# LayerNorm row sums out of the last PSUM addition, squares on ScalarE, and a new planned order, in a two-layer decoder trunk

## The chip, the cores and the metric

The kernel runs on one core of one Trainium2 chip. The metric is the device time of one launch in microseconds (us); a smaller one is better. The engines are TensorE (PE in the profile, its weight loads PEld), VectorE (DVE), ScalarE (ACT), GpSimd (POOL) and SyncE (SP, which issues nearly all transfers). "Span" is the time from the first to the last event of one profiled execution; that execution's own time is slightly longer.

## The reference, cut to what matters

512 tokens of width 1024 go through two layers. Layer 0 is a block-sparse attention with eight heads, layer 1 a gated DeltaNet with eight heads. Each layer modulates its input, projects it, mixes tokens, projects back, and ends in a LayerNorm over the residual:

```python
for i in range(2):
    mod = silu(c) @ ada_w[i] + ada_b[i]
    shift, scale, gate = split(mod, 3)
    h = x * (1 + scale) + shift
    y = moba_branch(h, ...) if i == 0 else gdn_branch(h, ...)
    x = layer_norm(4 ** 0.25 * x + gate * y, ln_g[i], ln_b[i])

def layer_norm(x, g, b):
    mu = mean(x); var = mean((x - mu) ** 2)
    return (x - mu) * rsqrt(var + 1e-5) * g + b
```

Everything is float32. The change is to how `mu` and `var` are computed, in both layer norms.

## The kernel before

**Tiling.** The residual `xn` stays in SBUF as four slices of 128 tokens (`st` = 0 to 3), each 128 partitions by 1024 numbers. A matmul in full precision is made of three passes with operands cut into a high and a low part (`wh`, `wl` of the weights, `hH`, `hL` of the activations). Projections land in PSUM banks of 128 x 512. `g2` is the half of the 1024 columns.

**The planner.** Every piece of work is a Python generator that yields the engine it wants, an estimated cost and the time at which its input is there. The class `Weave` picks the piece that can start first, and among equal ones that with the lowest rank. The table `PLACE` gives a rank to each piece by name; `RANK` holds ranks of groups, and six numbers `pool_...` by which work that may run on DVE or POOL is kept away from POOL: one twentieth of the number is added, in us, to POOL's end. `InOrder` fixes the order that results, so each engine runs a list that was decided ahead of the launch, and an instruction that waits holds all that stand behind it on its engine. The planner's estimates decide only the order; the chip decides the times.

**End of layer 0 and the norm between the layers.** `out0` (line 966) runs the output projection; slices 0 and 1 are made of two parts (`ya` for heads 0 to 5, `yb` for heads 6 and 7), slices 2 and 3 of one (`ya`). For each PSUM bank `evac` (line 884) multiplies by the gate row and adds to `xn`, both on DVE. `norm0` (line 922) then normalises a slice: `norm_stats` (line 905) runs `bn_stats` on each half of 512 columns on DVE, joins the two with `bn_aggr`, adds epsilon on DVE; `root` raises to the power of -0.5 on POOL; then two DVE operations, one for each half, subtract the mean and scale. `mod_t` transposes two normalised slices on PE (`h_ps`), applies layer 1's modulation (`ht`, on DVE and ACT) and cuts the result into `hH` (ACT) and `hL`. Its first half (`hf` = 0) is slices 0 and 1. `residual` afterwards scales and shifts `xn` for the residual of layer 1.

**Layer 1.** `proj1` takes the weights in the order of `order1`: z0 in two halves, q0, k0, v0, q1, v1 and so on, then the output projection in four parts (o0 to o3), each for two heads. `conv` runs a convolution over four taps and a SiLU on each projection (tiles `qc`, `kc`, `vc`), mostly on DVE. `decays` computes the decay factors, with a round trip through memory. `inverse(p)` starts from transposes of `kc` (`kt_ps`) and the decays and computes a triangular inverse for a pair of heads. `evac` adds each part of the output projection to `xn`: names `y0` to `y3`.

**The final norm.** `finish` (line 1776) handles a slice once all its parts are added. For slices 0 and 1 (`ACT_STATS = 2`) the sum is taken on ACT with a Copy that also writes out its row sum, and the squares with a Square pass on ACT; both dump their result in the slice's output buffer `f`. Slices 2 and 3 use `norm_stats` with `bn_stats` on DVE. Slices 0 to 2 are then normalised on ACT in halves and multiplied by g and shifted by b on DVE (or POOL); slice 3 takes two three-operand DVE operations for each half. `store` writes each half out.

Of the kernel before, what the change touches and what calls it, by code (L numbers as in the profile page):

```python
# [30 lines left out]
def flat(ap, dims, offset=0):  # L31
# [4 lines left out]
RANK = dict(pool_cut=42.445, pool_gate=32.272, pool_w=67.056, pool_mod=23.224, pool_res=0.0, pool_fin=0.0, fetch=22, kv0=50, qk0=45, kv00=40, cols2=20, mods=50, loads=25, evac0=96, conv0=17, decays=11, evac1=60, zs=49, conv=45, prep=8, resid=0, decay_f=67, inverse=4, inner=0, queries=40, values=94, recur=96, gated=7, keep0=43, norm0=37, mod_t=58, cut0=75, cut1=78)  # L36

PLACE = {
# [27 lines left out]
    "mod_t_1_2": -117.243, "mod_t_1_3": -977.754, "prep": 142.937, "residual": 134.202, "decays": -63.77,  # L66
# [30 lines left out]
}  # L97


def name_of(piece):  # L100

    code, given = piece.gi_code, piece.gi_frame.f_locals
    words = [code.co_name]
    for v in code.co_varnames[:code.co_argcount] + tuple(v for v in code.co_freevars if v == "st"):
        x = given.get(v)
        if isinstance(x, range):
            words.append(str(x[0]))
# [146 lines left out]
def act(n, ptr=0, acc=0):  # L254
    return 0.1 + 0.00083 * n + 0.09 * ptr + 0.1 * acc
# [12 lines left out]
def trunk(ctx: ExitStack, tc: tile.TileContext, x, c, ada_w, ada_b, ln_g, ln_b, moba_w_in, moba_w_out,  # L268
# [611 lines left out]
    pl.add(RANK["loads"], mod_loads())  # L880
    pl.add(100, proj0())


    def evac(o, st, g2, name, first_, e):
        gs = slice(g2 * 512, g2 * 512 + 512)
        if first_ is False:
# [982 lines left out]
```

## Time and profile before

| | us |
|---|---|
| median of three timed runs | 647.38 (646.84 to 647.98) |
| the profiled execution | 646.1 |
| its span | 644.4 |
| PE busy in the span | 614.2 |
| DVE busy | 484.1 |
| ACT busy | 346.2 |
| POOL busy | 46.7 |

All sums below are made against the profiled execution. Busy times of PE are modelled at the ends of matmuls. A duration printed for an operation is a little longer than the step by which its engine's queue advances, since the next one starts before the last one's end. Nearly all instructions carry one line number, that of the helper that records them, so the tiles' names tell them apart: `lnst`, `lnmv`, `lnve` are the statistics, `lnsq` the sums on ACT, `nb` the product of mean and reciprocal deviation, `fin` the buffer `f`.

### The profile page before, as it was taken

What the parts mean: (1) busy time and instruction counts of PE and PEld (TensorE: products, weight loads), DVE (VectorE), ACT (ScalarE), POOL (GpSimd) and SP (SyncE); (2) the same over time, 40 slices, a digit from 0 to 9 for tenths busy, and PEclk for the clock granted to TensorE, in tenths of its full rate; (3) what the DMA queues carried; (4) which work ended last, traced back from release to release, by engine and by line L of the source; (5) the groups of instructions that cost most, each with busy time, mean ns of one, the idle gap of its engine ahead of it and who ended that gap; (6) DMA issues with size and microseconds to landing.
All of it is one profiled execution on the core that took longest, in us unless ns stands there. A gap on an engine that the chain in (4) does not pass through costs nothing.

```text
span 644.4 us, 11258 instructions
## 1 busy us (share of the span) xinstructions
PE 614.2 (95%) x4214; PEld 519.0 (81%) x4214; DVE 484.1 (75%) x1099; ACT 346.2 (54%) x873; POOL 46.7 (7%) x65
## 2 busy tenths in 40 slices
PE   7999999999999999999889998899999999999992
PEld 6888788988888898888888886688878878887781
DVE  4796786775766468688889768857865986898877
ACT  1345764453544157204345595597589579745571
POOL 0000000000000000010300030010020021002011
PEclk8999999999999999999999998999999999999997
DMA  9995645455554335422313625344222423511203
GB/s 254 303 307 167 219 158 164 131 164 167 164 177 147 131 131 183 144 74 66 99 46 89 144 56 145 89 99 109 65 70 80 124 67 99 140 34 68 97 1 131
DMA packets 80969, 82.20 MB, mean 128 GB/s; under 512 B 8761, under 2 KB 67346, under 8 KB 80402
## 3 DMA queue, kind: packets, MB, share of 16 engines
q1 hardware_dynamic: 80834, 81.45, 43.3%
q8 instruction: 33, 0.54, 0.3%
q14 instruction: 22, 0.18, 0.1%
q10 hardware_dynamic: 80, 0.03, 0.0%
HBM read 78.82 MB, written 2.65 MB: 126 GB/s over the span
## 4 chain that ended last, share of the span: by engine, by line
PE 76%; DVE 9%; ACT 6%; DMA 4%; issue 2%; SPq 1%; DVEq 0%; ACTq 0%
PE z_ps L244 12%; PE y_ps L244 11%; PE gq_ps L244 7%; PE gk_ps L244 6%; PE v_ps L244 5%; PE k_ps L244 5%; PE q_ps L244 5%; PE gz_ps L244 4%; PE gv_ps L244 4%; PE s_ps L244 3%; PE o_ps L244 3%; DMA aw<-in_ada_w_dram 2%; PE os_ps L244 2%; PE kq_ps L244 2%; DVE xn L244 2%
## 5 line engine op out<-in xcount | busy, mean ns | idle before, releaser
L244 DVE SCALAR_TENSOR_TENSOR acc<-ga,cs,acc 128x512 f32<-128x512 f32 x56 | 40.3, 745 | 14.1 <-DMA ga<-in_ada_w_dram 14.1
L244 ACT ACTIVATE pr<-s_ps,nm 128x256 f32<-128x256 f32 (+1 forms) x48 | 20.6, 436 | 30.3 <-DVE nm L244 30.2
L244 DVE TENSOR_REDUCE nm<-s_ps 128x1 f32<-128x256 f32 (+1 forms) x64 | 22.0, 382 | 17.9 <-PE s_ps L244 17.9
L244 PE MATMUL gq_ps<-hH,wh_1q 128*128 128x512 f32 (+1 forms) x80 | 29.3, 366 | 0.0
L244 PE MATMUL gk_ps<-hH,wh_1k 128*128 128x512 f32 x64 | 26.8, 419 | 1.9 <-ACT wh_1k L244 1.3
L244 PE MATMUL v_ps<-wh_0v,hH 128*128 128x256 f32 x96 | 28.3, 295 | 0.0
L244 PE MATMUL gq_ps<-hL,wh_1q 128*128 128x512 f32 (+1 forms) x80 | 27.9, 348 | 0.0
L244 PE MATMUL gq_ps<-hH,wl_1q 128*128 128x512 f32 (+1 forms) x80 | 27.8, 348 | 0.0
L244 PE MATMUL z_ps<-hH,wh_0z 128*128 128x512 f32 x64 | 27.1, 424 | 0.7 <-ACT qT L244 0.7
L244 PE MATMUL y_ps<-wh_1o,ogh 128*128 128x512 f32 x64 | 27.1, 424 | 0.0
L244 PE MATMUL v_ps<-wh_0v,hL 128*128 128x256 f32 x96 | 27.1, 282 | 0.0
L244 PE MATMUL v_ps<-wl_0v,hH 128*128 128x256 f32 x96 | 27.1, 282 | 0.0
L244 PE MATMUL gk_ps<-hH,wl_1k 128*128 128x512 f32 x64 | 25.9, 404 | 1.3 <-DVE wl_1k L244 1.3
L244 DVE TENSOR_SCALAR nm<-nm 128x1 f32<-128x1 f32 x128 | 23.8, 189 | 4.1 <-ACT pr L244 1.1
L244 PE MATMUL gv_ps<-hH,wh_1v 128*128 128x512 f32 x64 | 26.6, 416 | 0.0
L244 DVE TENSOR_TENSOR xn<-xn,y_ps 128x512 f32<-128x512 f32 x34 | 23.2, 682 | 4.5 <-PE y_ps L244 4.2
L244 PE MATMUL gk_ps<-hL,wh_1k 128*128 128x512 f32 x64 | 25.5, 399 | 0.0
L244 PE MATMUL y_ps<-wh_0o,oH 128*128 128x512 f32 x64 | 25.5, 398 | 0.0
L244 PE MATMUL y_ps<-wl_1o,ogh 128*128 128x512 f32 x64 | 25.3, 395 | 0.0
L244 PE MATMUL y_ps<-wh_1o,ogl 128*128 128x512 f32 x64 | 25.2, 394 | 0.0
L244 PE MATMUL z_ps<-hL,wh_0z 128*128 128x512 f32 x64 | 25.2, 394 | 0.0
L244 PE MATMUL gv_ps<-hL,wh_1v 128*128 128x512 f32 x64 | 25.1, 392 | 0.0
(331 smaller groups left out, 1987.8 us busy)
## 6 DMA issues: line engine op xcount, KB each, us to landing
ga<-in_ada_w_dram SPq DMA_DIRECT2D x64, 256.0 KB
aw<-in_ada_w_dram SPq DMA_DIRECT2D x14, 512.0 KB
raw_0z<-in_moba_w_in_dram SPq DMA_DIRECT2D x8, 512.0 KB
raw_0o<-in_moba_w_out_dram SPq DMA_DIRECT2D x8, 512.0 KB
raw_1z<-in_gdn_w_in_dram SPq DMA_DIRECT2D x8, 512.0 KB
raw_1q<-in_gdn_w_in_dram SPq DMA_DIRECT2D x8, 512.0 KB
raw_1k<-in_gdn_w_in_dram SPq DMA_DIRECT2D x8, 512.0 KB
raw_1v<-in_gdn_w_in_dram SPq DMA_DIRECT2D x8, 512.0 KB
```

Of the source, the lines that this page charges most:

```text
L244: r = f(*args, **kwargs)
```

## The change

1. **Row sums.** The last addition into each half of a slice (`yb` or `ya` in layer 0, `y3` in layer 1) becomes a `scalar_tensor_tensor` that also writes the sum of its result along the row into a column of a small tile. For `y3` it waits until the other parts of that half have been added.
2. **Squares.** `norm_stats` no longer uses `bn_stats`. One small DVE operation makes minus the mean from the two sums; ACT squares the 1024 columns with that as bias and writes out the row sum; a small DVE operation makes the variance plus epsilon; POOL's power follows as before. The squares themselves are dumped: in the norm between the layers in columns 256 to 511 of `hL[:, 4:8]`, in the final norm in `f`.
3. **Normalising between the layers.** One half of each slice stays on DVE; the other half goes to ACT, with a new one-column product `nb`.
4. **The final norm** uses this for all four slices; the Copy on ACT and `ACT_STATS` are gone.
5. **The order.** All ranks in `PLACE` and the six `pool_...` numbers are new (`pool_cut` 42.4 to 3.0, `pool_gate` 32.3 to 53.6, `pool_mod` 23.2 to 14.8, `pool_res` 0 to 42.2, `pool_fin` 0 to 35.9), and `order1` takes v0 ahead of k0. No matmul is added or removed.

```diff
-    order1 = "z0 q0 k0 v0 q1 v1 k1 v2 k2 q2 z1 k3 q3 v3 z2 z3 o0 o1 o2 o3".split()
+    order1 = "z0 q0 v0 k0 q1 v1 k1 v2 k2 q2 z1 k3 q3 v3 z2 z3 o0 o1 o2 o3".split()
...
     def evac(o, st, g2, name, first_, e):
...
-        e = yield "DVE", dve(512), e
-        if first_:
+        final = name == ("yb" if st < 2 else "ya") or name == f"y{H // 2 - 1}"
+        if name == f"y{H // 2 - 1}":
+            e = max(e, (yield ("wait",) + tuple((n, st, g2) for n in sums_of(st)[:-1])))
+        e = yield "DVE", dve(512) + 0.08 * final, e
+        if final:
+            if (name, st) not in sums:
+                sums[name, st] = sm.tile([P, 6], F32, name="lnsq")
+            ve.scalar_tensor_tensor(xn[:, st, gs], xn[:, st, gs], ALPHA if first_ else 1.0, o, op0=ALU.mult, op1=ALU.add,
+                                    accum_out=sums[name, st][:, g2:g2 + 1])
+        elif first_:
...
-    def norm_stats(st, names):
-
-        stt = sm.tile([P, 2, 6], F32, name="lnst")
-        for q in range(2):
-            e = yield ("wait",) + tuple((n, st, q) for n in names)
-            e = yield "DVE", dve(512), e
-            ve.bn_stats(stt[:, q], xn[:, st, q * 512:(q + 1) * 512])
-        e = yield "DVE", 0.22, e
-        mv = sm.tile([P, 2], F32, name="lnmv")
-        ve.bn_aggr(mv, stt.rearrange("p a b -> p (a b)"))
...
+    def norm_stats(st, names, out_):
+
+        e = yield ("wait",) + tuple((n, st, q) for n in names for q in range(2))
+        sq = sums[names[-1], st]
+        e = yield "DVE", 0.1, e
+        ve.tensor_scalar(sq[:, 2:3], sq[:, 0:1], sq[:, 1:2], -1.0 / D, op0=ALU.add, op1=ALU.mult)
+        e = yield "ACT", act(1024, 1, 1), e
+        se.activation(out_, xn[:, st].rearrange("p (a b) -> p a b", b=256), AF.Square, bias=sq[:, 2:3], accum_out=sq[:, 3:4])
+        e = yield "DVE", 0.1, e
+        ve.tensor_scalar(sq[:, 4:5], sq[:, 3:4], 1.0 / D, LN_EPS, op0=ALU.mult, op1=ALU.add)
         key = "rstd", st, names
-        pl.add(0, root(key, vr[:, 1:2], vr[:, 0:1], e1))
-        return mv[:, 0:1], vr[:, 1:2], e, key
+        pl.add(0, root(key, sq[:, 5:6], sq[:, 4:5], e))
+        return sq[:, 2:3], sq[:, 5:6], e, key
 
     def norm0(st, names):
-        mu, rstd, e, key = yield from norm_stats(st, names)
+
+        nmu, rstd, e, key = yield from norm_stats(st, names, hL[:, 4:8, 256:512])
         e = yield "wait", key
-        for q in range(2):
-            qs = slice(q * 512, q * 512 + 512)
-            e = yield "DVE2", dve(512, 2, True), e - 0.2 * q
-            ve.tensor_scalar(xn[:, st, qs], xn[:, st, qs], mu, rstd, op0=ALU.subtract, op1=ALU.mult)
-        pl.mark(("xn", st), e)
+        e1 = yield "DVE", 0.1, e
+        nb = sm.tile([P, 1], F32, name="nb")
+        ve.tensor_mul(nb, nmu, rstd)
+        e = yield "DVE2", dve(512, 2, True), e
+        ve.tensor_scalar(xn[:, st, 0:512], xn[:, st, 0:512], nmu, rstd, op0=ALU.add, op1=ALU.mult)
+        e1 = yield "ACT", act(512, 2), e1
+        se.activation(xn[:, st, 512:1024], xn[:, st, 512:1024], AF.Identity, scale=rstd, bias=nb)
+        pl.mark(("xn", st), max(e, e1))
...
-        if st < ACT_STATS:
...
-            e = yield "ACT", act(1024, 0, 1), e
-            se.activation(f, xn[:, st], AF.Copy, accum_out=sq[:, 0:1])
...
-        else:
-            mu, rstd, e, key = yield from norm_stats(st, sums_of(st))
+        nmu, rstd, e, key = yield from norm_stats(st, sums_of(st), f.rearrange("p (a b) -> p a b", b=256))
```

## Rows read from the trace of the kernel before

**Rows 1.** The page: busy us, share, instructions; a group's busy, mean ns, idle.

```profile
PE 614.2 (95%) x4214; PEld 519.0 (81%) x4214; DVE 484.1 (75%) x1099; ACT 346.2 (54%) x873; POOL 46.7 (7%) x65
...
L244 DVE SCALAR_TENSOR_TENSOR acc<-ga,cs,acc 128x512 f32<-128x512 f32 x56 | 40.3, 745 | 14.1 <-DMA ga<-in_ada_w_dram 14.1
```

**Rows 2.** Table by stretch: length, busy us by engine, granted clock, DMA share, GB/s.

```profile
0.00:278.00 278.00, 271.97 (x1578) 232.86 (x1579) 191.74 (x473) 124.97 (x260) 2.16 (x9) 0.99 0.60 180
278.00:326.50 48.50, 44.62 (x259) 38.88 (x257) 41.37 (x76) 15.11 (x25) 8.44 (x12) 1.00 0.27 79
326.50:620.00 293.50, 285.91 (x2330) 238.25 (x2331) 231.84 (x508) 195.10 (x566) 31.08 (x38) 0.99 0.32 89
620.00:631.70 11.70, 11.66 (x52) 9.04 (x50) 9.82 (x28) 9.49 (x21) 3.60 (x5) 1.00 0.06 23
631.70:644.40 12.70, 0.00 (x0) 0.00 (x0) 9.33 (x17) 1.52 (x2) 1.38 (x2) 0.66 0.39 145
```

**Rows 3.** What PE waited for, whole span: us in total, times, longest.

```profile
PE X_ps L244 <- DVE UT L244: 2.7, 1, 2.7
PE h_ps L244 <- DVE xn L244: 2.1, 1, 2.1
```

**Rows 4.** Instructions on tile xn: count, minimum/median/maximum ns, first and last start.

```profile
L244 DVE TENSOR_TENSOR xn<-xn,y_ps x34: 648/686/690, 280.4 to 633.2; 128x512 f32<-128x512 f32 x34
...
L244 DVE BATCH_NORM_STATS2 lnst<-xn x12: 669/681/696, 281.6 to 634.4; 128x6 f32<-128x512 f32 x12
...
L244 DVE SCALAR_TENSOR_TENSOR xn<-xn,y_ps x8: 677/680/686, 266.6 to 308.9; 128x512 f32<-128x512 f32 x8
L244 DVE TENSOR_SCALAR xn<-xn,lnmv,lnve x8: 529/536/1480, 286.7 to 318.3; 128x512 f32<-128x512 f32 x8
...
L244 ACT ACTIVATE fin<-xn,nb,lnsq x4: 802/802/817, 626.5 to 629.2; 128x512 f32<-128x512 f32 x4
...
L244 ACT ACTIVATE fin<-xn,lnsq x2: 1152/1153/1154, 622.5 to 625.4; 128x1024 f32<-128x1024 f32 x2
L244 ACT ACTIVATION_READ_ACCUMULATOR fin<-xn,lnsq x2: 185/186/186, 623.5 to 626.4; 128x1 f32 x2
```

**Rows 5.** Timeline of DVE in the norm stretch: start us, us, instruction.

```profile
281.63 0.68 DVE L244 BATCH_NORM_STATS2 lnst<-xn 128x6 f32<-128x512 f32 x1
282.23 0.67 DVE L244 TENSOR_TENSOR xn<-xn,y_ps 128x512 f32<-128x512 f32 x1
```

**Rows 6.** Timeline of all engines, 308.9 to 321 us, slice 3.

```profile
308.95 0.68 DVE L244 SCALAR_TENSOR_TENSOR xn<-xn,y_ps 128x512 f32<-128x512 f32 x1
...
316.51 1.59 POOL L244 TENSOR_TENSOR xn<-xn,b0r 128x512 f32<-128x512 f32 x1
...
316.90 1.94 DVE L244 TENSOR_SCALAR xn<-xn,lnmv,lnve 128x512 f32<-128x512 f32 x2
...
318.89 1.86 PE L244 MATMUL h_ps<-ident,xn 128*128 128x128 f32 x15 [2.10 <-DVE xn L244]
```

**Rows 7.** Timeline of all engines, 619 us to the end, DVE and POOL.

```profile
624.60 0.69 DVE L244 TENSOR_TENSOR xn<-xn,y_ps 128x512 f32<-128x512 f32 x1 [0.49 <-PE y_ps L244]
...
636.35 0.15 DVE L244 TENSOR_SCALAR lnve<-lnmv 128x1 f32<-128x1 f32 x1
636.41 1.41 DVE L244 SCALAR_TENSOR_TENSOR fin<-xn,lnmv,g1r 128x512 f32<-128x512 f32 x2
636.57 0.98 POOL L244 TENSOR_TENSOR lnve<-lnve,mhalf 128x1 f32<-128x1 f32 x1 [4.47 <-DVE lnve L244]
...
640.39 0.68 DVE L244 TENSOR_TENSOR fin<-fin,b1r 128x512 f32<-128x512 f32 x1
```

**Rows 8.** Timeline of DVE, 343 to 372 us: the second kc and vc of pair 0.

```profile
352.85 0.68 DVE L244 SCALAR_TENSOR_TENSOR kc<-kc,pre 128x512 f32<-128x512 f32 x1
...
364.80 0.68 DVE L244 SCALAR_TENSOR_TENSOR vc<-vc,pre 128x512 f32<-128x512 f32 x1
```

**Rows 9.** Chain of work that ended last, in order of time: start us, us, what.

```profile
366.63 0.44 PE kt_ps L244 x4
```

More of the change, by code (lines that the diff above doesn't have):

```diff
@@ L32, in flat @@
     return bass.AP(tensor=ap.tensor, offset=ap.offset + offset, ap=dims)
-RANK = dict(pool_cut=42.445, pool_gate=32.272, pool_w=67.056, pool_mod=23.224, pool_res=0.0, pool_fin=0.0, fetch=22, kv0=50, qk0=45, kv00=40, cols2=20, mods=50, loads=25, evac0=96, conv0=17, decays=11, evac1=60, zs=49, conv=45, prep=8, resid=0, decay_f=67, inverse=4, inner=0, queries=40, values=94, recur=96, gated=7, keep0=43, norm0=37, mod_t=58, cut0=75, cut1=78)
+RANK = dict(pool_cut=3.02, pool_gate=53.593, pool_w=66.433, pool_mod=14.814, pool_res=42.179, pool_fin=35.925, fetch=22, kv0=50, qk0=45, kv00=40, cols2=20, mods=50, loads=25, evac0=96, conv0=17, decays=11, evac1=60, zs=49, conv=45, prep=8, resid=0, decay_f=67, inverse=4, inner=0, queries=40, values=94, recur=96, gated=7, keep0=43, norm0=37, mod_t=58, cut0=75, cut1=78)
 PLACE = {
[27 rows of a table removed]
-    "mod_t_1_2": -117.243, "mod_t_1_3": -977.754, "prep": 142.937, "residual": 134.202, "decays": -63.77,
[30 rows of a table removed]
[57 rows of a table added]
 }
@@ L881, in trunk, with sums_of @@
     pl.add(100, proj0())
+    sums = {}
+    def sums_of(st):
+        return tuple(f"y{p}" for p in range(H // 2) if p < 2 or (p, st) in last)
     def evac(o, st, g2, name, first_, e):
@@ L903, in root @@
         pl.mark(key, e)
-    def norm_stats(st, names):
-        stt = sm.tile([P, 2, 6], F32, name="lnst")
-        for q in range(2):
-            e = yield ("wait",) + tuple((n, st, q) for n in names)
-            e = yield "DVE", dve(512), e
-            ve.bn_stats(stt[:, q], xn[:, st, q * 512:(q + 1) * 512])
-        e = yield "DVE", 0.22, e
-        mv = sm.tile([P, 2], F32, name="lnmv")
-        ve.bn_aggr(mv, stt.rearrange("p a b -> p (a b)"))
-        vr = sm.tile([P, 2], F32, name="lnve")
-        e1 = yield "DVE", 0.08, e
-        ve.tensor_scalar_add(vr[:, 0:1], mv[:, 1:2], LN_EPS)
+    def norm_stats(st, names, out_):
[7 more added lines that the diff above has]
+        ve.tensor_scalar(sq[:, 4:5], sq[:, 3:4], 1.0 / D, LN_EPS, op0=ALU.mult, op1=ALU.add)
         key = "rstd", st, names
-        pl.add(0, root(key, vr[:, 1:2], vr[:, 0:1], e1))
-        return mv[:, 0:1], vr[:, 1:2], e, key
+        pl.add(0, root(key, sq[:, 5:6], sq[:, 4:5], e))
+        return sq[:, 2:3], sq[:, 5:6], e, key
     def norm0(st, names):
-        mu, rstd, e, key = yield from norm_stats(st, names)
+        nmu, rstd, e, key = yield from norm_stats(st, names, hL[:, 4:8, 256:512])
         e = yield "wait", key
-        for q in range(2):
-            qs = slice(q * 512, q * 512 + 512)
-            e = yield "DVE2", dve(512, 2, True), e - 0.2 * q
-            ve.tensor_scalar(xn[:, st, qs], xn[:, st, qs], mu, rstd, op0=ALU.subtract, op1=ALU.mult)
-        pl.mark(("xn", st), e)
+        e1 = yield "DVE", 0.1, e
[6 more added lines that the diff above has]
+        pl.mark(("xn", st), max(e, e1))
     def mod_t(hf, k2):
@@ L1769, in trunk @@
     fin = {}
-    ACT_STATS = 2
-    def sums_of(st):
-        return tuple(f"y{p}" for p in range(NP) if p < 2 or (p, st) in last)
     def finish(st):
         f = gd.tile([P, D], F32, name=f"fin{st}", tag=("kd", "vb", "Uf", "L")[st], bufs=1)
-        if st < ACT_STATS:
-            e = yield ("wait",) + tuple((n, st, q) for n in sums_of(st) for q in range(2))
-            sq = sm.tile([P, 4], F32, name="lnsq")
-            e = yield "ACT", act(1024, 0, 1), e
-            se.activation(f, xn[:, st], AF.Copy, accum_out=sq[:, 0:1])
-            e = yield "DVE", 0.1, e
-            ve.tensor_scalar_mul(sq[:, 1:2], sq[:, 0:1], -1.0 / D)
-            e = yield "ACT", act(1024, 1, 1), e
-            se.activation(f, xn[:, st], AF.Square, bias=sq[:, 1:2], accum_out=sq[:, 2:3])
-            e = yield "DVE", 0.1, e
-            ve.tensor_scalar(sq[:, 2:3], sq[:, 2:3], 1.0 / D, LN_EPS, op0=ALU.mult, op1=ALU.add)
-            key = "rstd", st
-            pl.add(0, root(key, sq[:, 3:4], sq[:, 2:3], e))
-            nmu, rstd = sq[:, 1:2], sq[:, 3:4]
-        else:
-            mu, rstd, e, key = yield from norm_stats(st, sums_of(st))
+        nmu, rstd, e, key = yield from norm_stats(st, sums_of(st), f.rearrange("p (a b) -> p a b", b=256))
         halves_ = [slice(q * 512, q * 512 + 512) for q in range(2)]
@@ L1796, in scaled @@
             e1 = yield "DVE2", dve(512, 1), e - 0.2
-            ve.scalar_tensor_tensor(f[:, qs], xn[:, st, qs], mu, fin["g"][:, qs], op0=ALU.subtract, op1=ALU.mult)
+            ve.scalar_tensor_tensor(f[:, qs], xn[:, st, qs], nmu, fin["g"][:, qs], op0=ALU.add, op1=ALU.mult)
             e1 = max(e1 - 0.2, (yield "wait", key))
@@ L1823, in finish @@
             nb = sm.tile([P, 1], F32, name="nb")
-            if st < ACT_STATS:
-                ve.tensor_mul(nb, nmu, rstd)
-            else:
-                ve.scalar_tensor_tensor(nb, mu, -1.0, rstd, op0=ALU.mult, op1=ALU.mult)
+            ve.tensor_mul(nb, nmu, rstd)
             for qs in halves_[:2 - on_ve]:
```

114 rows, old and new, of the table PLACE are left out of this document.

## The prediction

> **What bounds the kernel now.** I read the page's busy times first: PE works in 614.2 of 644.4 us, DVE in 484.1, ACT in 346.2 [rows 1]. So only the 30 us in which PE stands idle can be won, unless matmuls change, and no matmul does. The table by stretch says where they lie [rows 2]: 6.03 us before 278 us, 3.88 in the norm between the layers (278 to 326.5), 7.59 in the whole of layer 1, nothing just before PE's end, and 12.70 after its last matmul. PE's granted clock is 0.99 to 1.00 in the stretches with matmuls, the upper of its two levels, so the clock is no term.
>
> Next I asked what PE waited for. In the norm stretch the largest wait is 2.1 us of the transposes (h_ps) for DVE's xn [rows 3]; in layer 1 it is 2.7 us for the first triangular inverse [rows 3]. DVE is busy 41.37 of 48.5 us in the norm stretch, ACT 15.11 [rows 2]: the norm is limited by DVE's queue. That shows in one slice, st=3: its last addition ends at 308.95+0.68 = 309.6 us, and its normalisation ends at 316.90+1.94 = 318.84 [rows 6]. The steps between (two statistics, small operations, a power, two halves) would need about 3 us alone; the other 6 are queue. PE's transposes start at 318.89, after 2.10 us of idling [rows 6].
>
> After PE's end DVE is busy 9.33 us [rows 2], without a hole: the last operation ends at 640.39+0.68 = 641.07, and 641.07-631.70 is 9.37 [rows 7]. The queue is full from 624.60 on [rows 7]. So the tail is DVE's sum of work, not the last slice's latency, and the stores add the 3.3 us to 644.4.
>
> **The change, part by part.** Bn_stats goes: eight in the norm between the layers, four in the final one. Busy time is 681 ns each [rows 4], but the queue advances by 0.60 us (281.63 to 282.23) [rows 5], and that is what is saved.
>
> In the norm between the layers DVE loses 8x0.60 = 4.8 us and four of its eight scalings. Their median is 536 ns [rows 4], though one pair took 1.94 us beside a POOL addition of 1.59 [rows 6]; I count 0.53 each, 2.1 us. The aggregation and the epsilon step give way to two other one-column operations: no difference. Added are four products nb, a slot of 0.06 us each (636.35 to 636.41) up to a duration of 0.15 [rows 7], so 0.2 to 0.6 us, and eight outputs of row sums. No DVE operation of before writes a sum beside its result. Its price lies between nothing, if the sum comes with the last element, and an instruction of its own; the nearest row is ACT's, where the read of a sum is a separate 186 ns instruction [rows 4]. I take 0.12 each, about 1.0 us, between DVE's smallest slot 0.06 and ACT's 0.19; a gain is excluded, as the addition itself remains. The change from tensor_add to scalar_tensor_tensor costs nothing: the forms take 686 and 680 ns [rows 4]. Net: 6.9-0.4-1.0 = 5.5 us less DVE, bounds 4.8 and 6.7. ACT gets 4x(1.15+0.19+0.80) = 8.6 us [rows 4] in a stretch where it is idle for 33 [rows 2].
>
> ACT's row shows a read of the sum as an instruction of its own [rows 4]. The Trainium skill, "VectorE: DVE Perf Modes", section "Two Vector instructions with no wait between them", says that on DVE too an operation that writes out its accumulator is two instructions; no run here shows it yet, and by it the lower end, nothing, is out and the sum keeps 0.06 to 0.19 each.
>
> What is that worth on PE? Two slices, half of the 5.5 us, lie ahead of the h_ps transposes of st=2,3, so xn comes some 2.7 us sooner, against 2.10 us of waiting. The latency of one slice grows: Square and its read 1.34, two small operations and the crossings between engines replace about 0.9 us of statistics, roughly +1.0 us; it fits in the 6 us of queue. So the 2.10 go. The other 1.78 us of the stretch (3.88-2.10) are waits for the chain h_ps, ht, hH, hL, which the change leaves alone: I count none of them, and keep them as the outer bound. **Term 1: -2.1 us, bounds 0 and -3.9.**
>
> In the final norm slices 0 and 1 lose a Copy pass on ACT, which is not on the path. Slices 2 and 3 lose 4x0.60 = 2.4 us of DVE, inside the full queue, and gain four row-sum outputs, 0.5 us: net 1.9. Is the queue still full then? The last slice's own chain: the last addition cannot start before about 631.8; with 0.8 for it, 0.15, 0.1, 1.34, 0.1, 0.15 for the mean, Square and variance, 0.98 for POOL's power with 0.2 of crossings, and a pair of operations of 1.41 [rows 7], it ends at 637.0, some 2.2 us ahead of 641.07-1.9 = 639.2. DVE's sum stays the limit. One new order: Square writes the same buffer f as slice 3's first two products, so these wait for it; before they ran while the power was pending. The cover is st=2's four multiplications and additions (2.4 us). Without it the wait costs 1.3 us. **Term 2: -1.9 us, bounds -2.4 and -0.6.**
>
> ACT's Squares in the norm between the layers write hL[:, 4:8, 256:512] as a dump. Layer 0's matmuls on hL are over, mod_t overwrites it later, and PE's first half of layer 1 reads columns 0 to 255: nothing waits.
>
> The planned order is new everywhere: every rank, POOL's penalties, and v0 ahead of k0. POOL's penalty for cutting weights falls from 2.1 to 0.15 us, that for the residual rises from 0 to 2.1. Work moved to POOL relieves DVE by one slot but stretches what runs beside it: 1.94 us for a pair of scalings that take 1.07 by the median [rows 4, 6]. I set this at 0. The new order as a whole has no row. What it can reach is bounded above by PE's other gaps, 6.03+7.59 = 13.6 us [rows 2]; a third of them, 4 us, is what I allow either way, and 0 is the value I take, because both orders are written for the same chip. **Term 3: 0, bounds -4 and +4.** v0 ahead of k0: the second kc is now ready at 353.53, the second vc at 365.48 [rows 8], and the inverse's transposes (kt_ps) start at 366.63 [rows 9]. If kc takes vc's place it is still 1.15 us early; that is thin cover.
>
> Sum: -2.1-1.9 = -4.0 us on the profiled execution, 646.1 with a span of 644.4. The median of the timed runs, 647.38, lies 1.3 above it; I put the difference on the median: **643.4**.
>
> **Rivals.** *More than the sum (639.4).* The order planned for a freer DVE also closes a third of the 13.6 us of gaps and some of the 1.78: 643.4-4.0. For it: 2.7 of the gaps is one wait, for a chain that runs on DVE and ACT [rows 3]. Against: ACT gets work, and PE is full in most of layer 1.
>
> *Nothing arrives (647.4).* The statistics' chain replaces the wait it removes: in-order DVE stands at the variance step until Square is read, 1.34 us and two crossings, say 1.5. Eight such places could take 12 us, and five stood out in full eat the 5.5+1.9 us saved. For it: three more crossings in each slice. Against: 6 us of other work queue there.
>
> A variant is that the additions with a sum run at half rate, +0.60 us each. Eight cost 4.8 of the 5.5 us, the four in the tail 2.4 against 2.4 saved: 647 to 648. Against it stands that DVE took 745 ns for acc with two f32 sources in SBUF [rows 1], little more than an addition's 0.68 out of PSUM [rows 4]: no halving. The Trainium skill, "Vector Engine (DVE) Microarchitecture Reference", section "Points that are easy to get wrong", states such halving, for two non-bf16 sources in SBUF, since no port is left for the accumulator; here y_ps lies in PSUM, so by its own condition it would not apply.
>
> *Slower (651).* v0 ahead of k0 makes the first inverse late. Place: kt_ps at 366.63 [rows 9]. Its cover is 1.15 us. Two convolutions of a pair are 2x(3x0.75+0.68) = 5.9 us of DVE (a three-operand operation with a pointer takes 745 ns [rows 1], without one 0.68 [rows 4]); with v0's pair queued ahead of k0's, kc is 5.9-1.15 = 4.7 us late, with another half of a pair 7.7, and PE idles that much more: 643.4+7.7 = 651.1. It turns the sign when kc is over 4.0 us late, and is measurable from 5.3. For it: DVE is busy 231.84 of 293.5 us there [rows 2]. Against: kt_ps waits for the decays too, which an emptier DVE brings earlier, and PE has other products to run.
>
> **How the numbers follow.** Forecast (641 to 646) 0.45; more than the sum 0.20; nothing arrives 0.12 and half rate 0.05; slower 0.18. A measurement of this kernel tells 0.2%, 1.3 us, from no change. Faster: 0.45+0.20 = 0.65. Same: 0.12+0.05 = 0.17. Slower: 0.18. The range reaches 638, below the first rival's 639.4, and 650, just short of the slower rival's 651; about 0.07 and 0.11 lie outside.
>
> **What would show it.** In the norm stretch no BATCH_NORM rows, DVE busy about 5 us less than 41.4, the wait of h_ps for xn under 0.5 us, PE idle near 1.8. A separate row after each last addition, or a longer addition, settles the price of the sum. In the tail DVE still without a hole after PE's end, and about 7.5 us instead of 9.37 from PE's end to its last operation. Layer 1's PE idle near 7.6. Wrong it would be if DVE shows holes in front of the variance step, if kt_ps waits for kc, or if PE's idle time before 278 us or in layer 1 moves by more than 4.

## The result and the profile after

The changed kernel took 641.63 us at the median, the kernel before 647.11 beside it: ratio 0.9908, 95% interval 0.9888 to 0.9927. That is 5.5 us or 0.9% faster; 643.4 was predicted, and the range was 638 to 650. One of the four executions of the changed kernel took 1014.72 us at a granted clock of 0.557; it counts in the median and not in the ratio. The profiled execution took 641.54 us with a span of 639.8, against 646.1 and 644.4 before; so the two traces, 4.6 us apart, show a little less than the medians. The prediction had noted that the profiled execution of before lies 1.3 us under its median.

The first row is the page's line of busy times; the rows behind it are the table by stretch of the changed kernel (length, busy us of PE, PEld, DVE, ACT and POOL, granted clock, DMA share, GB/s). They answer to [rows 1, 2].

```profile
PE 612.9 (96%) x4218; PEld 518.6 (81%) x4218; DVE 475.5 (74%) x1106; ACT 355.3 (56%) x885; POOL 43.6 (7%) x62
```

```profile
0.00:278.00 278.00, 270.15 (x1573) 230.47 (x1574) 192.49 (x473) 126.48 (x260) 2.00 (x9) 0.99 0.61 183
278.00:326.50 48.50, 48.08 (x282) 42.42 (x280) 37.05 (x82) 22.79 (x37) 4.17 (x9) 1.00 0.22 61
326.50:620.00 293.50, 286.06 (x2331) 239.21 (x2330) 230.63 (x513) 195.95 (x571) 33.79 (x40) 0.99 0.32 89
620.00:631.70 11.70, 8.63 (x39) 6.55 (x37) 10.82 (x33) 9.58 (x17) 2.05 (x3) 0.99 0.18 68
631.70:639.80 8.10, 0.00 (x0) 0.00 (x0) 4.48 (x8) 0.47 (x2) 1.59 (x1) 0.50 0.43 162
```

DVE lost 8.6 us in all and 4.3 in the norm stretch, ACT gained 9.1 and 7.7. PE's idle time in the norm stretch fell from 3.88 to 0.42 us, before 278 us it rose from 6.03 to 7.85, and between 326.5 and 620 it stayed (7.59 to 7.44).

Fixed windows cut the two kernels at different work. So here are both, cut at the same work: the starts of the first layer-0 z matmul, of the first and last matmul of layer 0's output projection, of the last z matmul behind the norm and of the first matmul of layer 1's output projection, and PE's end. Same columns; before, then after.

```profile
0.00:65.50 65.50, 59.50 (x367) 53.55 (x367) 45.89 (x107) 24.26 (x33) 1.22 (x7) 0.95 0.97 257
65.50:259.90 194.40, 194.37 (x1124) 164.39 (x1125) 133.82 (x346) 97.54 (x224) 0.94 (x3) 1.00 0.51 162
259.90:307.00 47.10, 47.10 (x224) 39.09 (x224) 37.26 (x69) 10.85 (x18) 3.13 (x8) 1.00 0.28 84
307.00:331.60 24.60, 20.72 (x162) 19.81 (x161) 21.17 (x38) 7.81 (x14) 5.31 (x4) 1.00 0.21 65
331.60:569.30 237.70, 230.90 (x1839) 192.69 (x1837) 183.08 (x412) 168.34 (x489) 25.22 (x31) 0.99 0.36 96
569.30:631.70 62.40, 61.56 (x506) 49.51 (x505) 53.55 (x115) 35.86 (x97) 9.46 (x12) 1.00 0.15 56
```

```profile
0.00:67.00 67.00, 59.68 (x371) 53.31 (x371) 45.94 (x107) 24.59 (x33) 1.22 (x7) 0.97 0.93 252
67.00:261.80 194.80, 194.27 (x1123) 163.72 (x1123) 135.19 (x347) 98.45 (x224) 0.78 (x3) 1.00 0.51 164
261.80:309.10 47.30, 47.30 (x228) 39.38 (x226) 33.15 (x69) 15.97 (x26) 2.67 (x7) 1.00 0.26 76
309.10:329.80 20.70, 20.27 (x162) 19.78 (x161) 18.53 (x41) 10.65 (x18) 1.50 (x2) 1.00 0.26 78
329.80:568.10 238.30, 230.93 (x1843) 193.58 (x1842) 182.75 (x414) 167.87 (x489) 26.52 (x32) 0.99 0.36 96
568.10:628.60 60.50, 60.44 (x501) 48.87 (x499) 52.33 (x118) 34.98 (x94) 9.31 (x11) 1.00 0.17 58
```

Lengths, after minus before: +1.5, +0.4, +0.2, -3.9, +0.6, -1.9, and -1.5 behind PE's end (12.7 to 11.2): -4.6 in all. The norm between the layers gave 3.9, the tail 1.5, the end of layer 1 another 1.9 (its PE idle went from 0.8 to 0.06; the rest is work that lies ahead of this cut now, 501 matmuls in it and not 506), and the start took 1.5 back. From the start of the output projection to the last z matmul behind the norm DVE is busy 58.4 us before and 51.7 after, 6.7 less.

Now the norm itself. The timeline of the changed kernel's slice 3 (start us, us, what) answers to [rows 6]:

```profile
312.16 0.68 DVE L243 SCALAR_TENSOR_TENSOR xn<-xn,y_ps 128x512 f32<-128x512 f32 x1
312.76 0.08 DVE L243 DVE_READ_ACCUMULATOR xn<-xn,y_ps 128x1 f32 x1
312.76 0.69 DVE L243 TENSOR_TENSOR xn<-xn,g0r 128x512 f32<-128x512 f32 x1
...
313.61 1.16 ACT L243 ACTIVATE hL<-xn,lnsq 128x1024 fp32r<-128x1024 f32 x1 [0.81 <-DVE lnsq L243]
314.67 0.18 ACT L243 ACTIVATION_READ_ACCUMULATOR hL<-xn,lnsq 128x1 f32 x1
314.89 0.15 DVE L243 TENSOR_SCALAR lnsq<-lnsq 128x1 f32<-128x1 f32 x1
315.12 0.95 POOL L243 TENSOR_TENSOR lnsq<-lnsq,mhalf 128x1 f32<-128x1 f32 x1 [5.32 <-DVE lnsq L243]
316.51 0.15 DVE L243 TENSOR_TENSOR nb<-lnsq 128x1 f32<-128x1 f32 x1
316.58 0.54 DVE L243 TENSOR_SCALAR xn<-xn,lnsq 128x512 f32<-128x512 f32 x1
316.76 0.82 ACT L243 ACTIVATE xn<-xn,nb,lnsq 128x512 f32<-128x512 f32 x1 [1.64 <-DVE nb L243]
317.19 1.91 PE L243 MATMUL h_ps<-ident,xn 128*128 128x128 f32 x16
```

From the last addition's end to the slice's end it is 317.58-312.84 = 4.7 us, against 318.84-309.63 = 9.2 before [rows 6]. The transposes that had waited start 1.7 us earlier although layer 0's last output matmul starts 2.1 later (309.12, before 307.00): 3.8 us sooner relative to the work ahead, and without a wait. DVE fills the time in which Square runs with other slices' `g0r` and `b0r` operations, which need nothing from this slice.

Not all of the 9.2 us was DVE's own queue. Three of the DVE operations in them ran beside POOL's residual operations and took 1.73 us (309.55, a cut of weights), 1.35 (315.62, a `b0r` addition) and 1.94 (the pair of scalings [rows 6]); in the changed kernel such a cut takes 1.23 and such an addition 0.69, and in new_seq_old_mid below the pair takes 1.00. POOL has no residual operation there any more, which is the work of the new ranks and penalties and not of the statistics: stats_only below still has one there, order_only has none.

### The profile page after: what moved, and what is told of

It is laid out like the page before. It is cut to its first block, busy times and chain, and to the rows that moved or that the text cites. A ratio compares the mean times of both kernels' runs of the same rounds, so it can differ in the third digit from the quotient of the medians.

```text
span 639.8 us, 11280 instructions
## 1 busy us (share of the span) xinstructions
PE 612.9 (96%) x4218; PEld 518.6 (81%) x4218; DVE 475.5 (74%) x1106; ACT 355.3 (56%) x885; POOL 43.6 (7%) x62
## 4 chain that ended last, share of the span: by engine, by line
PE 70%; DVE 10%; ACT 9%; DMA 6%; issue 3%; SPq 1%; POOL 0%; POOLq 0%; DVEq 0%; ACTq 0%
PE z_ps L243 11%; PE y_ps L243 11%; PE gq_ps L243 6%; PE k_ps L243 5%; PE q_ps L243 5%; PE gk_ps L243 5%; PE gv_ps L243 5%; PE gz_ps L243 4%; PE v_ps L243 4%; DMA aw<-in_ada_w_dram 3%; PE s_ps L243 2%; PE o_ps L243 2%; PE os_ps L243 2%; DMA ga<-in_ada_w_dram 2%; ACT junk L243 2%
## 5 line engine op out<-in xcount | busy, mean ns | idle before, releaser
L243 DVE SCALAR_TENSOR_TENSOR acc<-ga,cs,acc 128x512 f32<-128x512 f32 x56 | 40.4, 745 | 14.9 <-DMA ga<-in_ada_w_dram 14.8
L243 PE MATMUL z_ps<-hH,wh_0z 128*128 128x512 f32 x64 | 26.9, 421 | 0.7 <-ACT qT L243 0.7
L243 PE MATMUL gv_ps<-hH,wl_1v 128*128 128x512 f32 x64 | 25.6, 400 | 0.0
```

Source lines behind the costliest of these rows:

```text
L243: r = f(*args, **kwargs)
```

## The experiments

One number serves for all: the "norm path", from the start of layer 0's first output matmul (y_ps, wh_0o) to the start of the last z matmul behind the norm (z_ps, wh_1z on hL), and the "tail", from the start of the last output matmul with wh_1o to the end of the span, both from the tiles' first and last starts.

| kernel | norm path, us | tail, us | ratio to before (95%) |
|---|---|---|---|
| before | 259.9 to 331.5: 71.6 | 631.0 to 644.4: 13.4 | 1 |
| after | 261.8 to 329.7: 67.9 | 628.0 to 639.8: 11.8 | 0.9908 (0.9888 to 0.9927) |
| stats_only | 260.1 to 328.4: 68.3 | - | 1.0553 (1.0505 to 1.0602) |
| order_only | 262.3 to 333.7: 71.4 | - | 1.0606 (1.0565 to 1.0647) |
| mid_norm_only | 262.3 to 330.1: 67.8 | 629.1 to 642.2: 13.1 | 0.9914 (0.9888 to 0.9939) |
| final_norm_only | 262.2 to 333.2: 71.0 | - | 1.0594 (1.0556 to 1.0632) |
| new_seq_old_mid | 261.8 to 332.6: 70.8 | 630.5 to 642.3: 11.8 | 0.9938 (0.9913 to 0.9963) |
| old_seq_new_stats | 260.1 to 332.3: 72.2 | 632.7 to 646.7: 14.0 | 1.0007 (0.9987 to 1.0028) |
| k0_first | 261.5 to 329.4: 67.9 | 628.5 to 640.4: 11.9 | 0.9890 (0.9863 to 0.9918) |
| before_start | 262.0 to 329.8: 67.8 | 628.7 to 640.6: 11.9 | 0.9865 (0.9836 to 0.9894) |
| no_row_sum | 261.8 to 329.7: 67.9 | 628.8 to 640.6: 11.8 | 0.9903 (0.9875 to 0.9930) |
| both_halves_dve | 261.2 to 330.0: 68.8 | 628.1 to 640.0: 11.9 | 0.9911 (0.9880 to 0.9941) |

### The two halves of the change, each alone

stats_only is the changed kernel with the ranks, penalties and `order1` of before; order_only is the kernel before with those of the changed kernel.

```diff
 # stats_only, from the changed kernel
-RANK = dict(pool_cut=3.02, ..., pool_res=42.179, pool_fin=35.925, ...)
+RANK = dict(pool_cut=42.445, ..., pool_res=0.0, pool_fin=0.0, ...)
-PLACE = {"warm": 139.505, ...}
+PLACE = {"warm": 135.873, ...}
-    order1 = "z0 q0 v0 k0 ...
+    order1 = "z0 q0 k0 v0 ...
```

> The new statistics in both norms, with the ranks, penalties and weight order of the kernel before. If the statistics themselves bring the gain: the wait of h_ps for xn (2.1 us) is gone, PE idle in the norm stretch under 1 us, PE's last matmul to the end under 11.7 us, time 3 to 5.5 us under before. If the new order brings it: within 1.3 us of before, and the freed DVE time shows as holes.

> The old statistics with the new ranks, penalties and v0 ahead of k0. If the statistics bring the gain: no gain, 0 to 3 us slower than before, since the first output projection starts 2 us later in the changed kernel than before. If the new order brings it: 3 us or more under before.

Measured: 684.47 and 687.21 us, before 648.76; 36 and 38 us slower. That is neither the statistics nor the new order as such: two kernels below, whose list of steps is frozen, mix old and new as well and take 645 and 649. Each rank was set for the costs of its own kernel; when the costs in the norm differ, the planner's list differs in all that comes after. What PE waited for in stats_only, then two windows that end with its last matmul (columns as above), then its output matmuls (ns, minimum/median/maximum):

```profile
PE og_ps L244 <- ACT ogn L244: 11.8, 9, 5.1
PE y_ps L244 <- ACT ogh L244: 2.9, 2, 1.4
```

```profile
569.00:632.00 63.00, 56.70 (x445) 44.53 (x446) 47.89 (x99) 32.71 (x95) 5.15 (x8) 0.89 0.28 78
632.00:676.70 44.70, 37.34 (x247) 28.34 (x245) 23.12 (x71) 20.11 (x58) 4.78 (x7) 0.89 0.10 36
```

```profile
L244 PE MATMUL y_ps<-wh_1o,ogh x64: 390/404/796, 577.3 to 675.8; 128*128 128x512 f32 x64
```

The gated outputs of layer 1 come late, PE stands idle (7.4 of its last 44.7 us), the mean granted clock sinks to 0.89, and some output matmuls take 796 ns where the median is 404. So these two times say nothing of the final norm's statistics. Ahead of layer 1 they do: the norm path is 68.3 us with the new statistics under the old ranks, and 71.4 with the old ones under the new ranks. The statistics, planned with their own costs, are worth 71.6-68.3 = 3.3 us under the old ranks and 71.4-67.9 = 3.5 under the new ones; the new ranks alone are worth 0.2.

order_only shows something else. With the residual off POOL its last slice is normalised 10.0 us behind the start of layer 0's last output matmul (before: 11.8, after: 8.5), and no transpose waits for xn. But 30 of the 48 matmuls of q0 lie ahead of those transposes there, where the kernel before has 27 and the changed kernel 15; too few are left behind them, and there PE waits instead:

```profile
PE z_ps L243 <- ACT hH L243: 1.5, 1, 1.5
```

So a wait for xn that is gone is not yet time that is won.

### One norm at a time

mid_norm_only has the new statistics between the layers and the old ones in the final norm; final_norm_only the reverse, both under the new ranks.

```diff
 # mid_norm_only: row sums only for the norm between the layers; finish() as before
-        final = name == ("yb" if st < 2 else "ya") or name == f"y{H // 2 - 1}"
+        final = name == ("yb" if st < 2 else "ya")
+    ACT_STATS = 2
```

> The changed kernel with the final norm's statistics as before (Copy and Square for slices 0 and 1, bn_stats for 2 and 3). If the two norms add up: 1.6 us slower than the changed kernel (its tail against that of before), so about 4 us under before, with 12.5 us or more from PE's last matmul to the end. If the tail is not DVE's sum of work but the last slice's chain: within 0.7 us of the changed kernel.

> The changed kernel with bn_stats and both scalings on DVE in the norm between the layers. If that norm is worth the 3.9 us of PE idle that went: 3 to 4.5 us slower than the changed kernel, 1 to 2.5 us under before, and PE idles 2 us or more at h_ps again. If the new order closed that gap: within 1 us of the changed kernel.

Measured: 643.22 us, and 686.27. In mid_norm_only the list is the changed kernel's up to the final norm, so its tail tells: 13.1 us against 11.8. The final norm's statistics are worth 1.3 us there, 1.6 together with the order; the changed kernel and the five variants below that have its final norm and nearly its list have tails of 11.8 to 11.9. The times of mid_norm_only and of the changed kernel cannot be told apart (ratios 0.9914 and 0.9908). final_norm_only fell like the two kernels above, since its costs in the norm between the layers differ from those that the ranks were set for; its time settles nothing, but its norm path of 71.0 agrees with order_only.

### The order held still

To part statistics and order without that fall, the planner's list was frozen: new_seq_old_mid keeps the changed kernel's list step for step and puts the old statistics into its norm between the layers; old_seq_new_stats keeps the list of before and puts the new instructions in their places, in both norms.

```diff
 # new_seq_old_mid, norm between the layers
-        ve.tensor_scalar(sq[:, 2:3], sq[:, 0:1], sq[:, 1:2], -1.0 / D, op0=ALU.add, op1=ALU.mult)
+        for q in range(2):
+            ve.bn_stats(stt[:, q], xn[:, st, q * 512:(q + 1) * 512])
+        ve.bn_aggr(mv, stt.rearrange("p a b -> p (a b)"))
+        ve.tensor_scalar_add(vr[:, 0:1], mv[:, 1:2], LN_EPS)
-        se.activation(out_, ..., AF.Square, bias=sq[:, 2:3], accum_out=sq[:, 3:4])
...
-        se.activation(xn[:, st, 512:1024], xn[:, st, 512:1024], AF.Identity, scale=rstd, bias=nb)
+        ve.tensor_scalar(xn[:, st, 512:1024], xn[:, st, 512:1024], mu, rstd, op0=ALU.subtract, op1=ALU.mult)
```

> The changed kernel with its planned sequence kept step for step; only in the norm between the layers the instructions are the old ones: two bn_stats, the aggregation and the epsilon step in the place of the mean, nothing in the place of ACT's Square, both scalings on DVE. If the new statistics themselves free PE there: 2 to 4 us slower than the changed kernel, h_ps waits for xn again, DVE 5 us busier in the stretch. If it is the sequence alone: within 1 us of the changed kernel.

> The kernel before with its planned sequence kept step for step and the new instructions put in: row sums from the last addition, Square on ACT at the step of the aggregation, the variance step right where the epsilon step was, half of each scaling on ACT. If removing DVE work is what counts, whatever the sequence: 3 to 5 us under before. If the sequence must know the new latency: DVE stands at the variance step about 1.3 us in up to six slices, the gain shrinks to 0 to 2 us.

Measured: 645.19 and 649.30 us, before 648.51. With the new list and the old statistics the wait of h_ps for DVE's xn is back, where [rows 3] has 2.1:

```profile
PE h_ps L243 <- DVE xn L243: 1.8, 2, 1.4
```

The norm path is 70.8: under the new list the statistics are worth 2.9 of the 3.7 us, and the list with the old statistics 0.8. In the time the ratios' intervals just overlap (0.9913 to 0.9963, the changed kernel's 0.9888 to 0.9927). In this kernel both bn_stats of a slice stand at one place of the list, so 2.9 may be a little much.

The old list with the new instructions wins nothing. What DVE and PE waited for in its norm (278 to 330 us), and a piece of its DVE timeline:

```profile
DVE lnsq L244 <- ACT hL L244: 6.2, 4, 3.4
```

```profile
PE h_ps L244 <- ACT xn L244: 2.9, 1, 2.9
```

```profile
317.28 1.59 POOL L244 TENSOR_TENSOR xn<-xn,b0r 128x512 f32<-128x512 f32 x1
```

```profile
317.67 1.21 DVE L244 TENSOR_TENSOR nb<-lnsq 128x1 f32<-128x1 f32 x1
318.80 0.53 DVE L244 TENSOR_SCALAR xn<-xn,lnsq 128x512 f32<-128x512 f32 x1
```

DVE has 6.6 us less to do between 278 and 326.5 (34.8 against 41.37 [rows 2]) and stands 6.2 us at the variance step, until ACT's Square is read: 3.4 of them at slice 2, and slice 3's last addition ends 4.1 us behind the start of layer 0's last output matmul instead of 2.6; another 0.5 at slice 3. Besides, POOL's residual operations lie beside the last slice, and the one-column product nb, 0.15 us without them, takes 1.21. How much each of the two took of the gain, this run does not part. In the changed list the residual is on DVE in front of that step, and DVE's timeline of slice 3 has no hole.

### v0 ahead of k0

```diff
-    order1 = "z0 q0 v0 k0 ...
+    order1 = "z0 q0 k0 v0 ...
```

> The changed kernel with k0 ahead of v0 as in the kernel before; ranks and penalties unchanged. If v0 ahead of k0 costs (kc late for the first inverse): 1 us or more under the changed kernel, and kt_ps starts earlier. If it has cover: within 0.7 us of the changed kernel, with kt_ps at the same time.

Measured: 642.1 us, before 648.51; the ratio of 0.9890 and the changed kernel's 0.9908 have overlapping intervals. The inverse's transposes start at 364.4 us, in the changed kernel at 364.7. In that one the second vc of pair 0 starts at 351.06 and the second kc at 362.99, the reverse of [rows 8], so kc takes the later place as feared and is still early enough (362.99+0.69 = 363.68). The swap does nothing that these runs can show.

### The start

before_start keeps the changed kernel's list but takes the first 62 us from that of before.

```diff
 # the list of steps: first 62 us from the kernel before, then the changed kernel's
-                if best is None or start < first - 1e-6:
-                    best, first, choice = p, start, (engine, cost)
+            best = next(p for p in self.pieces if name_of(p[2]) == name and p[3][0] not in ("slot", "wait"))
```

> The changed kernel with the sequence of the first 62 us (modulation, first activations and weights, their transfers) taken from the kernel before, step for step, and the rest of its own sequence kept step for step. If the 1.5 to 2 us by which the changed kernel reaches its first full projection later is the start's sequence and nothing further on needs it: 1.5 to 2 us under the changed kernel, some 7 us under before. If later waits take it up: within 0.7 us of the changed kernel.

Measured: 640.47 us. The first z matmul of layer 0 comes at 66.5 us instead of 67.0 (before: 65.5), but the output projection of layer 0 starts at 262.0, not earlier than 261.8. The trace shows no gain, and the intervals of the ratios overlap; whether the 1.5 us that the start lost can be had back stays open.

### The price of a row sum, and ACT's half

no_row_sum is the changed kernel without the sum outputs, with a mean made of two elements of the row in place of the sums; both_halves_dve puts the scaling that went to ACT back on DVE. In both the list stays as it is.

```diff
 # no_row_sum
-                                    accum_out=sums[name, st][:, g2:g2 + 1])
+                                    )
-        ve.tensor_scalar(sq[:, 2:3], sq[:, 0:1], sq[:, 1:2], -1.0 / D, op0=ALU.add, op1=ALU.mult)
+        ve.tensor_scalar(sq[:, 2:3], xn[:, st, 511:512], xn[:, st, 1023:1024], -1.0 / D, op0=ALU.add, op1=ALU.mult)
 # both_halves_dve
-        se.activation(xn[:, st, 512:1024], xn[:, st, 512:1024], AF.Identity, scale=rstd, bias=nb)
+        ve.tensor_scalar(xn[:, st, 512:1024], xn[:, st, 512:1024], nmu, rstd, op0=ALU.add, op1=ALU.mult)
```

> The changed kernel without the sum output of the sixteen last additions; the mean is made from two elements of the row instead, so the mean that it subtracts is wrong and all else, the order too, is as in the changed kernel. If a sum costs 0.12 us of DVE's queue, as the prediction took it, the norm between the layers loses 8x0.12 = 1.0 us of queue and the tail 0.5: 640.3 where the changed kernel has 641.6, ratio about 0.989 against 0.991. If its read hides in the queue (0.01 to 0.03 us each), at most 0.4 us is won over the whole kernel and the times are the same within 0.2%. If the additions with a sum ran slower (0.19 each), 2.1 us would be won.

> The changed kernel with the second half of each scaling in the norm between the layers back on DVE (tensor_scalar with subtracted mean and rstd) instead of ACT; the order is the planner's of the changed kernel, step for step. If DVE's queue sets the norm, four scalings of 0.53 us come back on it: DVE busy 37.1 goes to about 39.2 between 278 and 326.5, the last slice's xn is 1 to 2 us later, and the time is 642.6 to 643.6. If the latency of the chain sets it, the two halves of 0.53 one after the other take 0.25 us longer than 0.82 on ACT beside 0.54 on DVE: 641.8, the same as the changed kernel.

Measured: 641.92 and 642.67 us, before 648.35. DVE's timeline of no_row_sum, at the place of the first rows shown of slice 3:

```profile
312.18 0.68 DVE L243 SCALAR_TENSOR_TENSOR xn<-xn,y_ps 128x512 f32<-128x512 f32 x1
312.78 0.69 DVE L243 TENSOR_TENSOR xn<-xn,g0r 128x512 f32<-128x512 f32 x1
```

With the sum the next operation starts 312.76-312.16 = 0.60 us after the addition, without it 312.78-312.18 = 0.60. The read of 0.08 us has its own row and lies beside the next operation's start: here the sum costs nothing that the trace can show (at all sixteen places the next operation starts equally soon behind the addition, within 0.02 us, with the sum and without), and the time agrees (0.9903 and 0.9908).

With both halves on DVE the norm path is 0.9 us longer, 68.8, and PE waits for ACT's hH and a little for xn:

```profile
PE z_ps L243 <- ACT hH L243: 0.6, 1, 0.6
...
PE h_ps L243 <- DVE xn L243: 0.2, 1, 0.2
```

In the time that cannot be told from none. So of the 2.9 us of the statistics, some 0.9 is ACT's half and some 2.0, what is left, goes to the end of bn_stats.

## Why the prediction came out right, and which terms were off

**What bounds the kernel: right.** PE idled 30.2 us of its span before (644.4-614.2) and 26.9 after (639.8-612.9). The gain came out of the stretches that the prediction named, and DVE's queue was the main cause in the norm: with 6.7 us less in it, and an order that fits, the wait of h_ps is gone and PE's idle time with it. A part of what the prediction called queue, "the other 6", was DVE held up beside POOL, some 2.1 us by the three operations above.

**The sum: near in part by luck.** The norm gave 3.7 us where 2.1 was forecast, and the start took 1.9 where Term 3 had nothing; the two misses nearly cancel.

**Term 1, -2.1 us: too small.** It was 3.7 us, near the outer bound of -3.9: 2.9 by the statistics under the new list and 0.8 by the list. The step that failed is "The other 1.78 us of the stretch are waits for the chain h_ps, ht, hH, hL, which the change leaves alone: I count none of them". The chain was left alone, but what covers it was not. PE's waits of before in that stretch, and then after:

```profile
PE h_ps L244 <- DVE xn L244: 2.1, 1, 2.1
PE z_ps L244 <- ACT hH L244: 1.2, 1, 1.2
PE z_ps L244 <- DVE hL L244: 0.6, 2, 0.3
```

```profile
PE z_ps L243 <- DVE hL L243: 0.3, 1, 0.3
```

PE has some 5.8 us of q0's products (gq_ps) to run there. Before, it ran them ahead of the transposes while it waited for xn (from 313.28), and had 2.6 us left behind them (320.50 to 323.10) against the chain. After, xn was ready sooner, and 4.0 us were left (318.86 to 322.89). The same work can cover the wait for xn or the wait for the chain; 3.8 us sooner paid for both.

The parts of the term were sized fairly. "Some 2.7 us sooner" was 3.8 by the trace, list included; "5.5 us less DVE" was 6.7 from the output projection to the last z matmul, POOL's residual moved onto DVE included. "0.12 each" for the sum was nothing (no_row_sum). The variant at half rate is out (the prediction's row against it, acc with 745 ns, was no test, since acc writes no sum): the form with a sum takes 686 ns, the one without 684, as in these rows of tile xn of the changed kernel (count, minimum/median/maximum ns), which answer to [rows 4]:

```profile
L243 DVE TENSOR_TENSOR xn<-xn,y_ps x22: 676/684/690, 570.5 to 612.7; 128x512 f32<-128x512 f32 x22
L243 DVE SCALAR_TENSOR_TENSOR xn<-xn,y_ps x20: 666/686/689, 268.8 to 629.5; 128x512 f32<-128x512 f32 x20
L243 DVE DVE_READ_ACCUMULATOR xn<-xn,y_ps x16: 80/83/84, 283.1 to 630.1; 128x1 f32 x16
...
L243 ACT ACTIVATE hL<-xn,lnsq x4: 1137/1146/1155, 285.4 to 313.6; 128x1024 fp32r<-128x1024 f32 x4
L243 ACT ACTIVATION_READ_ACCUMULATOR hL<-xn,lnsq x4: 181/185/186, 286.4 to 314.7; 128x1 f32 x4
```

No row of bn_stats is left. The Trainium skill, "VectorE: DVE Perf Modes", section "Two Vector instructions with no wait between them", says that an operation that writes out its accumulator is two instructions; the trace agrees (the row DVE_READ_ACCUMULATOR, 83 ns). But the prediction drew from it that the lower end, nothing, was out, and that fell: the second instruction is there and takes no room in the queue.

**Term 2, -1.9 us: right, at -1.5 to -1.6.** Its picture of a tail without a hole was not quite right. DVE, ACT and POOL after the last addition, to be read beside [rows 7]:

```profile
629.47 0.68 DVE L243 SCALAR_TENSOR_TENSOR xn<-xn,y_ps 128x512 f32<-128x512 f32 x1
...
630.92 1.15 ACT L243 ACTIVATE fin<-xn,lnsq 128x1024 f32<-128x1024 f32 x1 [0.36 <-DVE lnsq L243]
...
632.61 0.15 DVE L243 TENSOR_SCALAR lnsq<-lnsq 128x1 f32<-128x1 f32 x1
...
632.84 1.59 POOL L243 TENSOR_TENSOR lnsq<-lnsq,mhalf 128x1 f32<-128x1 f32 x1 [4.75 <-DVE lnsq L243]
...
634.46 0.75 DVE L243 SCALAR_TENSOR_TENSOR fin<-fin,lnsq,b1r 128x512 f32<-128x512 f32 x1 [0.44 <-POOL lnsq L243]
...
635.91 0.75 DVE L243 SCALAR_TENSOR_TENSOR fin<-fin,lnsq,b1r 128x512 f32<-128x512 f32 x1
```

From PE's end (628.6) to DVE's last end (636.66) it is 8.0 us, not 7.5 and not 9.37. DVE's work there is 7.6 us, near the 7.5 that was forecast, and a hole of 0.44 comes on top: POOL's power took 1.59 where 0.98 was taken, beside DVE's large operations, and DVE stood for it. The 2.2 us that the last slice's chain was thought to be ahead are used up. The operation at 635.13 (`g1r`) needs only the mean and stands behind the one that waits for the power; whether it could fill the hole was not tried.

**Term 3, 0 us: about right as a sum, of parts with both signs.** Start +1.9 (to the output projection of layer 0), layer 1 and its output projection -1.2 (331.5 to 631.0 and 329.7 to 628.0), the list's share in the norm -0.8: together about -0.1. Where the start's 1.9 comes from stays open (before_start). With old statistics under the new list (new_seq_old_mid) layer 1 is as short, 297.9 us, so that gain is the list's.

**The rivals.** "More than the sum" has one half of what happened: the 1.78 that it named went, the gaps of layer 1 stayed. X_ps waited even longer for the inverse's UT, 4.4 us against 2.7 [rows 3], though it began 2.7 us sooner (405.6, before 408.3): PE came there earlier still. k0_first has the same 4.4, so it is not the swap. "Nothing arrives" is a true mechanism: old_seq_new_stats shows DVE standing 6.2 us at the variance step and the time of before, though POOL's residual has a share in that. What speaks against it is not that "6 us of other work queue there", as the prediction had it, but that the list places such work behind the mean step. "Slower" fell with the time: kc is later in the changed kernel, and k0_first shows that this has no price that can be seen.

## What to carry to other kernels

Where one engine's queue sets a stretch, a statistic that comes as a by-product of an operation that must run anyway, and a pass on an idle engine, are worth the queue that they free, but only if the fixed order is made anew for the longer chain: the same instructions in the old order won nothing. Count a wait that stands behind the one you remove as removable too, if the same work of PE covers both. And to find what one part of such a change is worth, freeze the order: ranks tuned to other costs give another program, here 36 to 38 us slower.

## What the hardware showed that was not expected

The accumulator's read on DVE is a row of 80 to 84 ns that takes no room in the queue, while ACT's read is 181 to 186 ns and holds the next operation up by 0.08 to 0.09 us (308.80 to 308.88 and 314.67 to 314.76 in the changed kernel). POOL's power on one column took from 0.55 us (309.25 in the changed kernel) to 1.59 (632.84), the longer ones beside large operations of DVE, and a one-column product on DVE took 1.21 us beside a POOL addition of 1.59 (old_seq_new_stats), where 0.15 is usual; it ended at 318.88, the addition at 318.87. In the kernels whose order had come apart PE's gaps cost more than their length: up to PE's last matmul the granted clock fell from 0.99 or 1.00 to 0.89 in the mean of a stretch in stats_only (from 632 us on) and 0.78 in order_only, between its two levels of 1.2 and 2.4 GHz, and PE was busy for 635 to 639 us with the matmuls that took 614 before and 613 in the changed kernel.
